# Ten raw weight buffers, five for low parts, and both weight sums loaded a pair of blocks ahead, in a decoder trunk on one core

## The chip, the core and the metric

The kernel runs on one core of a Trainium2 chip, in one launch. The time is that of the device, in microseconds (us), for the whole program. TensorE (PE) multiplies, VectorE (DVE), ScalarE (ACT) and GpSimd (POOL) do the elementwise work, and SyncE (SP) issues most DMAs. 16 DMA engines move the data.

## The reference

All is float32: 256 tokens, model width 1024, two layers, FFN width 2816. Cut to what matters:

```python
def swiglu(x, w_in, w_out):
    gate, up = jnp.split(x @ w_in, 2, axis=-1)
    return (jax.nn.silu(gate) * up) @ w_out

for layer in range(2):
    x = x + 0.5 * rms_norm(swiglu(rms_norm(x, g[0]), w_ffn_in[layer, 0], w_ffn_out[layer, 0]), g[1])
    h = rms_norm(x, g[2])
    h = mlstm_mixer(h, ...) if layer == 0 else diff_attention(h, k_sh, v_sh, ...)
    x = x + rms_norm(h, g[3])
    x = x + 0.5 * rms_norm(swiglu(rms_norm(x, g[4]), w_ffn_in[layer, 1], w_ffn_out[layer, 1]), g[5])
    gate = jax.nn.sigmoid(rms_norm(x, g[6]) @ w_ple_gate[layer])
    x = x + rms_norm((p[layer] @ w_ple_proj[layer]) * gate, g[7])
    if layer == 0:
        k_sh, v_sh = shared_kv(x, kv_norm, w_kv)      # rms_norm, then a 1024x2048 product
```

Each of the four FFNs reads 1024 x 5632 weights in and 2816 x 1024 out; mLSTM and attention read a few million more. Every weight is read from memory once or twice and used for 256 tokens only, so the weights pass through the core in a stream.

## The kernel before

**Split products.** TensorE multiplies in a format with fewer bits (fp32r). A weight block of 128 x 2048 floats (1 MB) is loaded into a *raw buffer* (`wraw`), ScalarE copies it to a *high part* (`whi`), VectorE subtracts that from the raw block and writes the *low part* (`wlo`); `parts` does both. The activations are split alike (`xh`, `xl`, for the hidden values `hh`, `hl`). A product is then three matmuls (`mm3`): high by high, low by high, high by low. There are `NRAW` = 9 raw buffers, and `NPART` = 6 each for high and for low parts. Each buffer takes 8 KB of every partition.

**Pairs of blocks.** `block_pair` computes the products of two input-weight blocks at once with seven instead of eight products, in the manner of Strassen and Winograd. `src` is the pair's first block, `src2` its second, each in two halves of 1 MB. Two of the seven weights are sums that the DMA makes: t3 = `src2[0] + src2[1]` and u1 = `src[0] + src2[0]`. For each, SyncE loads the one term (the *base load*) into a raw buffer, and then GpSimd issues an *adding load*, a DMA that adds the other term to what is there; it has to wait until the base has landed. The three blocks b11 = `src[0]`, b21 = `src[1]` and b22 = `src2[1]` are loaded plainly, and VectorE adds two more weights in place, wt2 = b11 + t3 and wt4 = b21 + b11. So a pair holds five raw buffers, and each is free when its last reader on VectorE is done. The products come in the order w11, w21, wt2, wu1, then wt3 and w22, then wt4.

**Where the pairs are.** An FFN has 11 input blocks (`NJ`); the first FFN makes pairs at 5, 7 and 9, the other three at 1, 3, 5, 7 and 9. `ffn` walks through them; between two pairs it issues the output products of the pair before (`stage_out`, weights `ffn_out`). The pairs of mLSTM (two calls) know nothing of one another. Within an FFN the next pair's t3 is loaded by the current call, between its loads of b22 and of the output weights, and handed on; u1 is loaded by the pair itself.

**What sets the order.** Nothing is issued as the code stands. The class `Notes` records all instructions, and `play` lays them in time with a model of costs: always the one that can start first, among those that could start at once the one that stands first in the code (with `is_urgent` ones before others on ACT, DVE and POOL, and SyncE strictly in the code's order among those whose buffers exist). Buffers of a kind are given out in the code's order, too, at the time when the model says that an older one is free. The result is a fixed order on each engine. `later` sets when a load counts as landed in the model, and so, when its readers may be put in place:

```python
        def later(q, t):
            t += 810 + SLACK if q.kw.get("accum_op") is not None else 180 + LATE
```

`LATE` is 600 ns, `SLACK` 3000 ns. The chip doesn't know this model: there each engine takes its instructions in that order, and waits by semaphores for what is really late. SyncE waits in the same way: a load whose buffer isn't free holds up all loads behind it. Because all instructions are issued in one place, all have the line L432 (L433 after the change).

Of the kernel before, what the change touches and what calls it, by code (L numbers as in the profile page):

```python
# [10 lines left out]
F32R = mybir.dt.float32r  # L11
# [5 lines left out]
P = 128  # L17
# [7 lines left out]
PEN = 30  # L25
MARGIN = 300
SLACK = 3000
LATE = 600
LANES = 8
DEPTH = 2  # L30
HA = 4
# [2 lines left out]
BIG = 2.0 ** 100  # L34
GKV = 8
ATT = 8
NRAW = 9
NPART = 6
NX = 7
NSG = 3  # L40
NH = 3
# [393 lines left out]
def trunk(nc, a):  # L435
# [34 lines left out]
        nc.vector.scalar_tensor_tensor(dst_lo, src, gc, dst_hi.bitcast(F32), op0=ALU.mult, op1=ALU.subtract)  # L470

    def part():
        return T([P, 2048], "whi", NPART, F32R), T([P, 2048], "wlo", NPART, F32R)


    def pair(*shape):
# [237 lines left out]

    def block_pair(xts, xf, src, src2, use, end=False, between=None, nxt=None, t3=None):
        def load(src, plus=None):
            raw = T([P, 2048], "wraw", NRAW)
            nc.sync.dma_start(raw, src)  # L720
            if plus is not None:
                nc.gpsimd.dma_start(raw, plus, accum_op=ALU.add)
            return raw

        def parts(raw):
            p_ = part()
            split(*p_, raw)
            return p_

        def add(out, v0, v1):  # L730
            nc.vector.tensor_tensor(out, v0, v1, op=ALU.add)
            return parts(out)

        nc.is_urgent = False
        if t3 is None:
            t3 = load(src2[0], src2[1])
        u1 = load(src[0], src2[0])
        b11 = load(src[0])
        w11 = parts(b11)
        b21 = load(src[1])  # L740
        w21 = parts(b21)
        wt2 = add(b11, b11, t3)
        wu1 = parts(u1)
        wt3 = parts(t3)
        b22 = load(src2[1])
        t3 = load(nxt[1][0], nxt[1][1]) if nxt else None
        w22 = parts(b22)
        wt4 = add(b21, b21, b11)
        nc.is_urgent = True

        def times(acc_, x_, w, more):
            for kk in range(4):
                c = slice(kk * 512, (kk + 1) * 512)
                mm3([acc_], x_[0][:, kk, :], x_[1][:, kk, :], [w[0][:, c]], [w[1][:, c]],
                    not more and kk == 0, kk == 3, more)

        def quarter(t, q):
            return xts[t][0][:, q:q + 4, :], xts[t][1][:, q:q + 4, :]

        def held(acc_):  # L760
            c = piece()
            nc.scalar.activation(c, acc_, AF.Copy)
            return c

        ax, ay = acc_in(), acc_in()
        times(ax, quarter(0, 0), w11, False)
        p1 = held(ax)
        times(ay, quarter(0, 4), w21, False)
        nc.vector.tensor_tensor(p1, ay, p1, op=ALU.add)
        use(0, 0, p1)  # L770
        if between:
            between()
        s1, s2, s3, n4 = xf() if callable(xf) else xf
        times(ax, s2, wt2, True)
        u2 = held(ax)
        az = acc_in()
        times(az, s1, wu1, False)
        z5 = held(az)
        if end:
            times(az, n4, w22, True)  # L780
            nc.vector.tensor_tensor(u2, az, u2, op=ALU.subtract)
            use(1, 0, u2)
        times(ax, s3, wt3, True)
        u3 = held(ax)
        nc.vector.tensor_tensor(z5, z5, u3, op=ALU.subtract)
        if not end:
            times(az, n4, w22, True)
            nc.vector.tensor_tensor(u2, az, u2, op=ALU.subtract)
        use(1, 1, z5)
        times(ax, quarter(1, 4), wt4, True)  # L790
        if not end:
            use(1, 0, u2)
        use(0, 1, ax)
        return t3

    def ffn(l, f, xts, rs, xfs, epilogue, first=None):
        acc = [None, None]
        wi, wo, hT = dict(enumerate(first)) if first else {}, {}, {}  # L800
        res = [None, None]
        gbc = []
        win = a["ffn_in"][l, f]


        def hidden(j, t, src):
            h = T([P, 256], "sg", NSG)
            nc.scalar.activation(h, src[:, :256], AF.Silu, scale=rs[t])
            nc.vector.scalar_tensor_tensor(h, src[:, 256:], rs[t], h, op0=ALU.mult, op1=ALU.mult)
            hh = T([P, 2, P], "hh", NH, F32R)  # L810
            hl = T([P, 2, P], "hl", NH, F32R)
            pt = trp()
            for i in range(2):
                nc.tensor.transpose(pt[:, i * P:(i + 1) * P], h[:, i * P:(i + 1) * P], ident)
            split(hh, hl, pt[:, :256].rearrange("p (k t) -> p k t", t=P))
            hT[j, t] = hh, hl

        def stage_in(j, t):
            if j not in wi:
                wi[j] = in_weights(win[j], m=2 if j < 2 or j == NJ - 1 else 1)  # L820
            pi = acc_in()
            in_block(pi, xts[t], wi[j])
            hidden(j, t, pi)

        def stage_out(j, t):
            if j not in wo:
                wo[j] = [weight(a["ffn_out"][l, f, j], m=2 if j < 2 or j == NJ - 1 else 1)]
            if acc[t] is None:
                acc[t] = acc_out()
            hh, hl = hT.pop((j, t))  # L830
            for i in range(2):
                out_chunk(acc[t], hh[:, i, :], hl[:, i, :], wo[j], i,
                          j == 0 and i == 0, j == NJ - 1 and i == 1)

        def end(t):
            post(t, acc[t], gbc[0], 0.5)
            res[t] = epilogue(t)

        xf = []
        first_n = 1 if first else 0  # L840
        if first:
            pis = [acc_in() for _ in range(NT)]
            for k in range(KD):
                hi, lo = wi[0][k // 4]
                c = slice(k % 4 * 512, k % 4 * 512 + 512)
                for t in range(NT):
                    mm3([pis[t]], xts[t][0][:, k, :], xts[t][1][:, k, :], [hi[:, c]], [lo[:, c]], k == 0, k == KD - 1)
            for t in range(NT):
                hidden(0, t, pis[t])
        starts = PAIRS[2 * l + f]  # L850
        items = []
        j = 1 if first else 0
        while j < NJ:
            items.append((j, j + 1) if j in starts else (j,))
            j += len(items[-1])

        begin = 0
        while len(items[begin]) == 1 and begin < (1 if first else 2):
            begin += 1

        split_begin = begin == 1 and not first
        for t in range(1 if split_begin else NT):
            for (j,) in items[:begin]:
                stage_in(j, t)
        last = [0] * first_n + [j for i in items[:begin] for j in i]
        for t in range(1 if split_begin else NT):
            stage_out(last[0], t)
        last = last[1:]

        def late():  # L870
            stage_in(0, 1)
            stage_out(0, 1)

        def all_forms():
            if not xf:
                xf.extend(forms(xfs, urgent=split_begin))
            return xf

        def both(item, **kw):
            return block_pair(xts, all_forms, win[item[0]], win[item[1]], lambda b, t, src: hidden(item[b], t, src), **kw)  # L880

        t3 = None
        for n, item in enumerate(items[begin:-1]):
            if len(item) == 2:
                nxt = items[begin + n + 1]
                t3 = both(item, between=late if split_begin and n == 0 else None, t3=t3,
                          nxt=[win[i] for i in nxt] if len(nxt) == 2 else None)
            else:
                for t in range(NT):
                    stage_in(item[0], t)  # L890
            for t in range(NT):
                for i in last:
                    stage_out(i, t)
            last = item
        item = items[-1]
        gbc.append(load_gbc(a["norm_g"][l, 4 * f + 1]))
        if len(item) == 1:
            j, = item
            stage_in(j, 0)
            for i in last:  # L900
                stage_out(i, 0)
            stage_out(j, 0)
            end(0)
            stage_in(j, 1)
            for i in last:
                stage_out(i, 1)
            stage_out(j, 1)
            end(1)
        else:

            both(item, end=True, t3=t3)
            for t in range(NT):
                for i in last:
                    stage_out(i, t)
            for t in range(NT):
                for i in item:
                    stage_out(i, t)
                end(t)
        return res
# [583 lines left out]
```

## Time and profile before

| | |
|---|---|
| time before, three runs | 1010.15, 1009.94, 1007.89 us; median 1009.94 |
| time of the profiled execution | 1006.51 us, 3.43 under the median |
| its span in the profile | 1004.7 us, TensorE's clock 0.999 of full speed |
| instructions | 12418 |
| data moved | 274.68 MB, 273 GB/s over the span |
| TensorE, VectorE, ScalarE, GpSimd busy | 987.2, 893.1, 697.9, 88.6 us |

How to read it: busy time is the time in which an engine executes; loads of weights into TensorE (PEld) overlap its matmuls. `<-` reads "made from": `whi_0r<-wraw` is a high part made from a raw buffer. Names of buffers end in a number of the buffer, which tells nothing of what is in it. In brackets stands the idle time of the engine just ahead of the instruction and what ended it. PEclk is the clock that the throttle granted TensorE; the DMA share is that of the 16 engines, and can read slightly above 1. By the tiles of the timeline the stages lie roughly so, in us from the start of the span: first FFN of layer 0 to 200, mLSTM to 300, second FFN to 472, gate and shared K/V to 495, first FFN of layer 1 to 700, attention to 785, last FFN to 966, gate to the end; the next stage's first work overlaps the one before.

### The profile page before, as it was taken

What the parts mean: (1) busy time and instruction counts of PE and PEld (TensorE: products, weight loads), DVE (VectorE), ACT (ScalarE), POOL (GpSimd) and SP (SyncE); (2) the same over time, 40 slices, a digit from 0 to 9 for tenths busy, and PEclk for the clock granted to TensorE, in tenths of its full rate; (3) what the DMA queues carried; (4) which work ended last, traced back from release to release, by engine and by line L of the source; (5) the groups of instructions that cost most, each with busy time, mean ns of one, the idle gap of its engine ahead of it and who ended that gap; (6) DMA issues with size and microseconds to landing.
All of it is one profiled execution on the core that took longest, in us unless ns stands there. A gap on an engine that the chain in (4) does not pass through costs nothing. (4 is left out here: it accounts for less than half of the span.)

```text
span 1004.7 us, 12418 instructions
## 1 busy us (share of the span) xinstructions
PE 987.2 (98%) x4636; PEld 803.2 (80%) x4636; DVE 893.1 (89%) x909; ACT 697.9 (69%) x924; POOL 88.6 (9%) x126
## 2 busy tenths in 40 slices
PE   9999999999999999999999999999999999999997
PEld 7888888887787788888887788788888887888886
DVE  6977998788999999998899899998985999999983
ACT  8747767577847867595767767676776787767662
POOL 0000000100131000001120000000002300000010
PEclk9999999999999999999999999999999999999999
DMA  9999778765699999966799999965657898998721
GB/s 345 418 333 335 234 245 301 241 191 186 252 292 339 290 337 311 311 252 221 293 280 321 349 335 326 311 248 222 232 216 230 241 330 285 286 306 283 282 84 42
DMA packets 45860, 274.68 MB, mean 273 GB/s; under 512 B 5481, under 2 KB 5865, under 8 KB 16105
## 3 DMA queue, kind: packets, MB, share of 16 engines
q1 hardware_dynamic: 39752, 231.69, 60.1%
q0 software_dynamic: 5760, 41.95, 20.8%
q8 instruction: 36, 0.59, 0.2%
q10 hardware_dynamic: 288, 0.27, 0.1%
q14 instruction: 24, 0.19, 0.0%
HBM read 263.40 MB, written 10.49 MB: 273 GB/s over the span
## 5 line engine op out<-in xcount | busy, mean ns | idle before, releaser
L432 DVE TENSOR_TENSOR wraw<-wraw,wraw 128x2048 f32<-128x2048 f32 x40 | 91.3, 2282 | 0.2
L432 ACT ACTIVATE whi_0r<-wraw 128x2048 fp32r<-128x2048 f32 (+2 forms) x49 | 77.8, 1597 | 11.7 <-DMA wraw<-in_mlstm_in 3.8
L432 ACT ACTIVATE whi_2r<-wraw 128x2048 fp32r<-128x2048 f32 (+1 forms) x48 | 79.4, 1663 | 7.7 <-PE accI L432 3.5
L432 ACT ACTIVATE whi_1r<-wraw 128x2048 fp32r<-128x2048 f32 (+2 forms) x51 | 78.2, 1542 | 7.4 <-PE accO L432 4.1
L432 ACT ACTIVATE whi_5r<-wraw 128x2048 fp32r<-128x2048 f32 (+1 forms) x44 | 71.7, 1641 | 15.6 <-PE accI L432 11.5
L432 ACT ACTIVATE whi_4r<-wraw 128x2048 fp32r<-128x2048 f32 (+1 forms) x45 | 73.7, 1648 | 6.0 <-PE accO L432 2.6
L432 ACT ACTIVATE whi_3r<-wraw 128x2048 fp32r<-128x2048 f32 (+1 forms) x45 | 74.1, 1648 | 4.9 <-DMA wraw<-in_ffn_in 3.3
L432 ACT ACTIVATE att<-accI 128x512 f32<-128x512 f32 x80 | 47.5, 593 | 34.0 <-PE accI L432 33.7
L432 POOL DMA_DIRECT2D wraw<-in_ffn_in x36 | 32.0, 888 | 426.3 <-DMA wraw<-in_ffn_in 363.3
L432 DVE TENSOR_TENSOR wlo_0r<-wraw,whi_2r 128x2048 fp32r<-128x2048 f32 (+1 forms) x25 | 48.3, 1942 | 1.3 <-ACT whi_2r L432 1.3
L432 DVE TENSOR_TENSOR wlo_3r<-wraw,whi_1r 128x2048 fp32r<-128x2048 f32 (+1 forms) x25 | 48.4, 1941 | 1.1 <-ACT whi_1r L432 1.1
L432 DVE TENSOR_TENSOR wlo_2r<-wraw,whi_2r 128x2048 fp32r<-128x2048 f32 (+1 forms) x21 | 43.7, 2080 | 4.6 <-ACT whi_2r L432 4.5
L432 DVE TENSOR_TENSOR wlo_1r<-wraw,whi_1r 128x2048 fp32r<-128x2048 f32 (+2 forms) x26 | 44.4, 1709 | 3.5 <-ACT whi_1r L432 3.4
L432 DVE TENSOR_TENSOR wlo_1r<-wraw,whi_0r 128x2048 fp32r<-128x2048 f32 (+1 forms) x23 | 46.0, 2005 | 0.4 <-ACT whi_0r L432 0.2
L432 DVE TENSOR_TENSOR wlo_0r<-wraw,whi_0r 128x2048 fp32r<-128x2048 f32 (+2 forms) x24 | 44.1, 1839 | 0.8 <-ACT whi_0r L432 0.6
L432 DVE TENSOR_TENSOR wlo_5r<-wraw,whi_4r 128x2048 fp32r<-128x2048 f32 (+1 forms) x23 | 44.0, 1912 | 0.3 <-ACT whi_4r L432 0.3
L432 DVE TENSOR_TENSOR wlo_4r<-wraw,whi_4r 128x2048 fp32r<-128x2048 f32 (+1 forms) x22 | 43.6, 1991 | 0.3 <-ACT whi_4r L432 0.3
L432 POOL TENSOR_TENSOR sm<-sm,mhalf 128x1 f32<-128x1 f32 (+2 forms) x40 | 32.5, 813 | 109.0 <-DVE sm L432 106.5
L432 DVE TENSOR_TENSOR wlo_2r<-wraw,whi_3r 128x2048 fp32r<-128x2048 f32 (+1 forms) x22 | 41.7, 1894 | 0.3 <-ACT whi_3r L432 0.3
L432 DVE TENSOR_TENSOR wlo_4r<-wraw,whi_5r 128x2048 fp32r<-128x2048 f32 (+1 forms) x22 | 41.4, 1894 | 0.0
L432 POOL TENSOR_SCALAR sm<-sm 128x1 f32<-128x1 f32 x32 | 16.9, 527 | 261.8 <-ACT sg L432 261.8
L432 ACT ACTIVATE sg<-accI,sm 128x256 f32<-128x256 f32 x34 | 16.0, 471 | 32.9 <-PE accI L432 24.2
(617 smaller groups left out, 3041.4 us busy)
## 6 DMA issues: line engine op xcount, KB each, us to landing
wraw<-in_ffn_in SPq DMA_DIRECT2D x102, 1024.0 KB, 9.5
wraw<-in_ffn_out SPq DMA_DIRECT2D x44, 1024.0 KB, 9.3
wraw<-in_ffn_in POOLq DMA_DIRECT2D x36, 1024.0 KB, 12.0
wraw<-in_mlstm_in SPq DMA_DIRECT2D x14, 1024.0 KB, 6.9
wraw<-in_ple_gate SPq DMA_DIRECT2D x8, 1024.0 KB, 5.5
wraw<-in_w_kv SPq DMA_DIRECT2D x8, 1024.0 KB, 5.1
home<-wraw SPq DMA_DIRECT2D x28, 256.0 KB, 4.1
wraw<-home SPq DMA_DIRECT2D x14, 512.0 KB, 3.4
```

The lines of the kernel that those rows point to most:

```text
L432: getattr(getattr(self.nc, eng), name)(*args, **kw)
```

## The change

Four things are changed together. There is one raw buffer more (ten) and one low-part buffer less (five; `NLOW` is new, high parts keep six): the memory is the same. A plain load counts as landed 400 ns later in the planner's model (`LATE` 1000). And in `block_pair` the sums of the next pair are no longer t3 alone, loaded ahead of `w22 = parts(b22)`, but t3 and u1 together, loaded behind it. mLSTM's pairs pass no next pair on, and so there only the numbers have an effect.

```diff
-LATE = 600
+LATE = 1000
-NRAW = 9
+NRAW = 10
 NPART = 6
+NLOW = 5
     def part():
-        return T([P, 2048], "whi", NPART, F32R), T([P, 2048], "wlo", NPART, F32R)
+        return T([P, 2048], "whi", NPART, F32R), T([P, 2048], "wlo", NLOW, F32R)
-    def block_pair(xts, xf, src, src2, use, end=False, between=None, nxt=None, t3=None):
+    def block_pair(xts, xf, src, src2, use, end=False, between=None, nxt=None, ahead=None):
...
-        if t3 is None:
-            t3 = load(src2[0], src2[1])
-        u1 = load(src[0], src2[0])
+        t3, u1 = ahead or (load(src2[0], src2[1]), load(src[0], src2[0]))
         b11 = load(src[0])
         w11 = parts(b11)
         b21 = load(src[1])
...
         b22 = load(src2[1])
-        t3 = load(nxt[1][0], nxt[1][1]) if nxt else None
         w22 = parts(b22)
+        ahead = (load(nxt[1][0], nxt[1][1]), load(nxt[0][0], nxt[1][0])) if nxt else None
         wt4 = add(b21, b21, b11)
...
-        return t3
+        return ahead
```

(`ffn` hands `ahead` on in the place of `t3`.) The instructions are the same ones, 12418 before and after; what moves is their place on each engine, and the buffers that they use. Three places follow; `wraw_8_85` is a raw buffer, the second number only an address in the order.

SyncE at the last pair of FFN one of layer 1, before: t3, two blocks of output weights, the gains of a norm, two halves of a parked residual (`home`), u1, then b11, b21 and b22.

```order
L432 DMA wraw_8_85<-in_ffn_in 128x2048
L432 DMA wraw_5_82<-in_ffn_out 128x2048
L432 DMA wraw_7_84<-in_ffn_out 128x2048
L432 DMA wraw_6_83<-in_norm_g 128x1024
L432 DMA wraw_2_79<-home_2_88 128x1024
L432 DMA wraw_2_79<-home_3_89 128x1024
L432 DMA wraw_1_78<-in_ffn_in 128x2048
L432 DMA wraw_4_81<-in_ffn_in 128x2048
L432 DMA wraw_3_80<-in_ffn_in 128x2048
L432 DMA wraw_5_82<-in_ffn_in 128x2048
```

And after:

```order
L433 DMA wraw_0_76<-in_ffn_in 128x2048
L433 DMA wraw_1_77<-in_ffn_in 128x2048
L433 DMA wraw_4_80<-in_ffn_out 128x2048
L433 DMA wraw_7_83<-in_ffn_out 128x2048
L433 DMA wraw_9_85<-in_norm_g 128x1024
L433 DMA wraw_5_81<-home_2_88 128x1024
L433 DMA wraw_5_81<-home_3_89 128x1024
L433 DMA wraw_8_84<-in_ffn_in 128x2048
L433 DMA wraw_3_79<-in_ffn_in 128x2048
L433 DMA wraw_6_82<-in_ffn_in 128x2048
```

u1 has moved up five places, right behind t3; b11, b21 and b22 keep theirs.

VectorE from the attention to the start of the last FFN, before (`xl`: low part of the activations; `sm4` and `mhalf`: the statistics of the softmax's norm; `accO`: an accumulator; the sums into `wraw_8_85` and `wraw_5_82` are the residual):

```order
L432 TENSOR_TENSOR wlo_4r_75<-wraw_0_77,whi_5r_70 128x1024
L432 TENSOR_TENSOR wlo_1r_72<-wraw_4_81,whi_0r_65 128x1024 x2
L432 SCALAR_TENSOR_TENSOR sm4_4_138<-sm4_2_136,sm4_0_134 128x2
...
L432 SCALAR_TENSOR_TENSOR xl_2r_115<-tr_0_97,sub_0_164,xh_2r_108 128x512
L432 SCALAR_TENSOR_TENSOR wraw_5_82<-wraw_8_85,sm1_4_160,wraw_5_82 128x512 x2
L432 TENSOR_TENSOR wlo_2r_73<-wraw_2_79,whi_3r_68 128x1024
L432 TENSOR_TENSOR att_4_102<-tr_0_97,gcol_0_130 128x512
L432 TENSOR_TENSOR att_1_99<-accI_2_92,gcol_0_130 128x512
L432 TENSOR_TENSOR xl_0r_113<-att_4_102,xh_0r_106 128x512
L432 TENSOR_TENSOR xl_4r_117<-att_1_99,xh_4r_110 128x512
L432 TENSOR_TENSOR wlo_2r_73<-wraw_2_79,whi_3r_68 128x1024
```

And after:

```order
L433 TENSOR_TENSOR wlo_0r_71<-wraw_7_83,whi_1r_66 128x1024 x2
L433 SCALAR_TENSOR_TENSOR sm4_4_138<-sm4_2_136,sm4_0_134 128x2
...
L433 SCALAR_TENSOR_TENSOR xl_2r_115<-tr_0_97,sub_0_164,xh_2r_108 128x512
L433 SCALAR_TENSOR_TENSOR wraw_1_77<-wraw_4_80,sm1_4_160,wraw_1_77 128x512 x2
L433 TENSOR_TENSOR wlo_2r_73<-wraw_3_79,whi_4r_69 128x1024
L433 TENSOR_TENSOR att_7_105<-tr_0_97,gcol_0_130 128x512
L433 TENSOR_TENSOR att_2_100<-accI_1_91,gcol_0_130 128x512
L433 TENSOR_TENSOR xl_0r_113<-att_7_105,xh_0r_106 128x512
L433 TENSOR_TENSOR xl_4r_117<-att_2_100,xh_4r_110 128x512
L433 TENSOR_TENSOR wlo_2r_73<-wraw_3_79,whi_4r_69 128x1024
L433 TENSOR_TENSOR wlo_3r_74<-wraw_0_76,whi_0r_65 128x1024 x2
```

The low part `wlo_1r` of before, ahead of the softmax's statistics, is the `wlo_2r` of after, one half behind the residual sum and one behind `xl`; what was there before (`wlo_2r` of before) follows it as `wlo_3r`.

GpSimd in the attention, before: an adding load (for t3), two powers of the softmax's norm, the next adding load (for u1).

```order
L432 TENSOR_TENSOR sm4_1_135<-sm4_13_147,mhalf_0_133 128x4
L432 DMA wraw_6_83<-in_ffn_in 128x2048
L432 TENSOR_TENSOR sm4_3_137<-sm4_4_138,mhalf_0_133 128x2
L432 TENSOR_TENSOR sm4_5_139<-sm4_9_143,mhalf_0_133 128x2
L432 DMA wraw_1_78<-in_ffn_in 128x2048
```

And after:

```order
L433 TENSOR_TENSOR sm4_1_135<-sm4_13_147,mhalf_0_133 128x4
L433 DMA wraw_9_85<-in_ffn_in 128x2048
L433 DMA wraw_5_81<-in_ffn_in 128x2048
L433 TENSOR_TENSOR sm4_3_137<-sm4_4_138,mhalf_0_133 128x2
L433 TENSOR_TENSOR sm4_5_139<-sm4_9_143,mhalf_0_133 128x2
```

The second adding load, with its wait for the base to land, now stands ahead of the two powers.

More of the change, by code (lines that the diff above doesn't have):

```diff
@@ L880, in both @@
             return block_pair(xts, all_forms, win[item[0]], win[item[1]], lambda b, t, src: hidden(item[b], t, src), **kw)
-        t3 = None
+        ahead = None
         for n, item in enumerate(items[begin:-1]):
@@ L885, in ffn @@
                 nxt = items[begin + n + 1]
-                t3 = both(item, between=late if split_begin and n == 0 else None, t3=t3,
-                          nxt=[win[i] for i in nxt] if len(nxt) == 2 else None)
+                ahead = both(item, between=late if split_begin and n == 0 else None, ahead=ahead,
+                             nxt=[win[i] for i in nxt] if len(nxt) == 2 else None)
             else:
@@ L909, in ffn @@
         else:
-            both(item, end=True, t3=t3)
+            both(item, end=True, ahead=ahead)
             for t in range(NT):
```

## The prediction

> **What bounds the kernel now.** I read the page's busy shares and slices first, then the busy time of TensorE by stretch, then the chain of waits, then the timeline at each place where TensorE stood idle.
>
> ```profile
> PE 987.2 (98%) x4636; PEld 803.2 (80%) x4636; DVE 893.1 (89%) x909; ACT 697.9 (69%) x924; POOL 88.6 (9%) x126
> DMA  9999778765699999966799999965657898998721
> ```
>
> TensorE works 98% of the span. Both programs hold the same instructions, so its 987.2 us stay, and the change can only touch the 17.5 us in which it stands still. The busy time by stretch (us, PE busy and count, granted clock, DMA share, GB/s) says where these lie:
>
> ```profile
> 0.00:25.00 25.00, 23.12 (x98) 1.00 0.92 344
> ...
> 225.00:300.00 75.00, 72.71 (x339) 1.00 0.72 243
> 300.00:325.00 25.00, 24.93 (x114) 1.00 1.02 332
> 325.00:350.00 25.00, 22.73 (x100) 1.00 0.96 301
> ...
> 500.00:575.00 75.00, 73.89 (x341) 1.00 0.97 314
> 575.00:650.00 75.00, 75.00 (x338) 1.00 0.97 319
> 650.00:675.00 25.00, 24.01 (x109) 1.00 0.65 254
> ...
> 825.00:875.00 50.00, 48.48 (x216) 1.00 0.93 276
> 875.00:975.00 100.00, 100.00 (x461) 1.00 0.71 249
> 975.00:1004.70 29.70, 22.34 (x123) 0.96 0.17 60
> sum 1004.70, PE 987.17; mean PE 75.94
> ```
>
> 1.88 us go at the start and 7.36 us in the tail, where no pair of blocks is loaded: the change leaves both. That leaves 17.53 - 9.24 = 8.29 us: mLSTM 2.29, the start of the second FFN of layer 0 (300 to 350) 2.34, the start of the first FFN of layer 1 (500 to 575) 1.11, its last pair (650 to 675) 0.99, the start of the last FFN (825 to 875) 1.52, and 0.04 elsewhere. Two of the five are on the chain of waits with a landing:
>
> ```profile
> 635.70 2.21 DVE wraw L432
> 637.93 10.85 DMA wraw<-in_ffn_in
> 648.80 1.92 ACT whi_3r L432
> ...
> 835.68 10.50 DMA wraw<-in_ffn_in
> 846.26 1.92 ACT whi_3r L432
> ```
>
> VectorE's sum of two blocks ends and frees a raw buffer, the load that waited for it is issued, it lands 10.9 us later, and ScalarE rounds it. So at these places the supply of raw buffers sets the time of a product, and a tenth buffer or another order of loads bears on it. Where it is not the load, it is VectorE:
>
> ```profile
> 290.00:350.00 60.00, 58.76 (x56) 1.00 1.00 310
> 500.00:550.00 50.00, 48.44 (x53) 1.00 0.96 298
> ...
> 764.00:783.00 19.00, 8.10 (x16) 1.00 1.01 294
> 783.00:852.00 69.00, 66.95 (x64) 1.00 0.89 282
> ```
>
> These are VectorE's busy times (same columns): 98% and 97% at three FFN starts, but idle for more than half of the stretch just ahead of the last one, in the attention.
>
> **The change part by part.** All is counted against the profiled execution, 1006.51 us, of which the span is 1004.7; the median of the three runs is 1009.94, 3.43 above it, and I add that at the end.
>
> *The tenth raw buffer.* SyncE's queue is in order and its loads of weights stand waiting for a buffer most of the time, and so a tenth buffer lets each load go one release earlier:
>
> ```profile
> SPq L432 <- DVE wraw L432: 143.3, 48, 17.1
> ...
> L432 DVE TENSOR_TENSOR wraw<-wraw,wraw 128x2048 f32<-128x2048 f32 x40 | 91.3, 2282 | 0.2
> ```
>
> (VectorE's releases by sums alone held the queue 143.3 us in 48 waits; a sum takes 2.28 us, and so does a low part.) One release is therefore worth at least 2.28 us of an earlier issue where VectorE runs without a gap, and nothing where PE isn't waiting for a load.
>
> *mLSTM, second pair of blocks: forecast -2.0.* The pair's first block waits for its load:
>
> ```profile
> 220.07 0.86 POOL L432 DMA_DIRECT2D wraw<-in_mlstm_in  x1 [2.92 <-DMA wraw<-in_mlstm_in]
> 221.02 8.93 SPq L432 DMA_DIRECT2D wraw<-in_mlstm_in  x3
> ...
> 233.10 1.92 ACT L432 ACTIVATE whi_0r<-wraw 128x2048 fp32r<-128x2048 f32 x1 [3.83 <-DMA wraw<-in_mlstm_in]
> ...
> 235.53 0.69 DVE L432 TENSOR_TENSOR att<-att,att 128x512 f32<-128x512 f32 x1 [3.76 <-ACT att L432]
> ```
>
> It was issued at 221.0, 1 us behind an adding load of POOL, and ScalarE could start at 233.10, after 3.83 us of waiting; VectorE then waited 3.76 us. Issued one release earlier, the block comes 2.3 us earlier or more and goes ahead of that adding load, not behind it. The new order of TensorE also has the products there in unbroken groups of twelve matmuls, where the old one cut them up to fill the wait. Bounds: 0 (another operand is late, at the same time) to -2.29 (all of the stretch's idle time). I take -2.0, near the far end, since the wait of 3.83 us is longer than the idle time it makes. There is nothing loaded ahead in this stage, so the other half of the change has no part in it.
>
> *Last pair of the first FFN of layer 1: forecast -1.0.* Here both weight sums are loaded a pair ahead. SyncE's order moves the load of u1 five places up, past two blocks of the output weights and three small loads; the two block loads b11 and b21 then stand in front of nothing but their own buffers.
>
> ```profile
> 636.75 0.86 POOL L432 DMA_DIRECT2D wraw<-in_ffn_in  x1 [17.47 <-DMA wraw<-in_ffn_in]
> ...
> wraw<-in_ffn_in SPq DMA_DIRECT2D x102, 1024.0 KB, 9.5
> wraw<-in_ffn_in POOLq DMA_DIRECT2D x36, 1024.0 KB, 12.0
> wraw<-in_mlstm_in POOLq DMA_DIRECT2D x4, 1024.0 KB, 12.4
> ...
> q1 hardware_dynamic: 39752, 231.69, 60.1%
> q0 software_dynamic: 5760, 41.95, 20.8%
> ```
>
> The critical b21 (637.93, 10.85 us) ran beside the adding load of u1 (636.75), against a median of 9.5 us from issue to landing. An adding load takes 20.8/41.95 = 0.50% of the engines per MB, a plain one 60.1/231.69 = 0.26%: 1.9 times. Loaded a pair ahead, u1's adding load is out of b21's way, and b21 itself goes a release (2.28 us) earlier. Either is more than the 0.99 us of idle time. The two output blocks that u1 passes are wanted only after the pair. Bounds 0 to -0.99; I take -1.0.
>
> *Second FFN of layer 0: forecast -0.5.*
>
> ```profile
> 340.69 0.50 PE L432 MATMUL accI<-whi_1r,xh_1r 128*128 128x512 f32 x1 [1.14 <-ACT whi_1r L432]
> ...
> 342.08 0.50 PE L432 MATMUL accI<-wlo_4r,xh_2r 128*128 128x512 f32 x1 [0.89 <-DVE wlo_4r L432]
> ```
>
> TensorE waits first for a high part, then for a low part, with VectorE 98% busy for 60 us. An earlier landing can't give VectorE time; what the change does is swap two low parts of that pair and take one sum forward. Bounds 0 to -2.34, and I stay near the low end, because VectorE's rows decide here and its work is the same.
>
> *First FFN of layer 1, its start: 0.* DMA stands at 0.97 and VectorE at 97%. The tenth buffer brings loads forward by one release, the fifth low buffer in place of the sixth holds low parts back by one. Bounds -1.11 to +2.28 (one low part uncovered).
>
> *Five low buffers, the last FFN: forecast +0.5.* A low part can be written only when TensorE has read an older one out. With a lead of many products that costs nothing; at the start of the last FFN there is none: TensorE waits for low parts that VectorE has just made.
>
> ```profile
> 764.68 2.50 DVE L432 TENSOR_TENSOR wlo_1r<-wraw,whi_0r 128x1024 fp32r<-128x1024 f32 x2
> ...
> 850.68 0.50 PE L432 MATMUL accO<-wlo_5r,hh_1r 128*128 128x512 f32 x1 [1.15 <-DVE wlo_5r L432]
> ```
>
> The two halves of the sixth low part (2.50 us at 764.68, in the attention's idle stretch of VectorE, 8.10 of 19 us busy) now stand behind the residual sums at 783, in the stretch that is 97% busy. So 2.5 us of work come into 69 us that had 2.05 us free. On the other side the loads of this FFN come one release earlier and a sum that was made early is put off, which is what TensorE waited for at 841 to 852. Bounds -1.52 (all idle time gone) to +2.5 (the shifted work uncovered). The middle is +0.5, and I take that.
>
> *POOL in the attention: 0.* The adding load of the second weight sum moves ahead of two small powers:
>
> ```profile
> 767.85 0.71 POOL L432 TENSOR_TENSOR sm<-sm,mhalf 128x2 f32<-128x2 f32 x1 [5.04 <-DVE sm L432]
> ...
> 769.84 0.92 POOL L432 DMA_DIRECT2D wraw<-in_ffn_in  x1
> ```
>
> POOL waits there for the base load to land. If that lands after 767.85 the softmax of the attention waits with it; if not, the issue of 0.92 us fits into the 5.04 us that POOL idled. The base's load goes up the queue by three or more releases, so I put it at nothing; its price if the cover is gone is 0.92 us and what the base is late.
>
> Everywhere else (25 to 225, 350 to 500, 575 to 650, 675 to 825, 875 to 975) TensorE has no gap: earlier loads hide there, as the moved loads of output weights do. *The later landings in the order* (the 1000 in place of 600) only set which instruction stands first on each queue; their effect is in the moves above.
>
> Sum: -2.0 - 1.0 - 0.5 + 0 + 0.5 + 0 = -3.0. 1006.51 - 3.0 = 1003.5 for an execution like the profiled one; 3.43 more is 1006.9.
>
> **The rivals.** *Larger gain.* All 8.29 us between start and tail go, as each place is fed earlier: 1009.94 - 8.29 = 1001.7; half of the remainder beyond my sum gives 1004.3. For it: every wait of TensorE listed above is short (0.9 to 1.2 us), less than one release. Against: VectorE at 97 to 98%.
>
> *Nothing gained.* VectorE sets the FFN starts and an earlier landing turns into a longer wait in a buffer; only the last pair of layer 1 and part of mLSTM pay, and the last FFN loses as much: within 1.5 us of 1009.9, 1008.4 to 1011.4.
>
> *Slower: the low parts.* At each of the three FFN starts with VectorE at 97 to 98% (290, 500, 783), one low part of 2.28 us that was made in a gap ahead of it falls into the full stretch. This decides as soon as the stretch has less than 2.28 us free, and they have 1.24 of 60, 1.56 of 50 and 2.05 of 69 us (the rows above). If TensorE pays for each in full, 3 x 2.28 = 6.8; less the 2.0 and 1.0 that the loads still bring, 1013.7. Against it: the low parts' lead outside these starts, and that two of three places have sums pushed back in exchange.
>
> *Slower: the adding loads.* Both weight sums ahead mean two adding loads back to back in front of the next pair's blocks. An adding load costs 0.208 x 1004.7 / 40 = 5.2 us of all engines (20.8% for the 40 of them, by the rows of 36 in the FFN and 4 in mLSTM at 1 MB each), a plain one 2.6. Where engines are full (1.02 at 300 to 325) the blocks behind land up to 5.2 us later. One release of 2.28 us is gained, 2.9 lost; at the three starts with no lead 3 x 2.9 = 8.7 at most, half of it on the path +4.4, less the 1.0 of the last pair: 1013.3. It speaks against it that u1 was loaded in front of b11 before as well, and only its place among other loads moves. The Trainium skill, page "DMA: Bandwidth & Descriptors", section "Queues, rings and completion order", says that each engine takes packets in turn from the queues that have work. By that rule an early adding load slows every plain load beside it, wherever it is put. The trace agrees at 637.93, where b21 took 10.85 us beside an adding load; by that rule the last pair would gain and a start with full engines lose, which is this rival's 1013.3.
>
> **How the numbers follow.** 0.3% is 3.0 us, about what a measurement of this kernel tells from no change; the line for faster is 1006.9, for slower 1013.0. The forecast (1005.4 to 1008.4) 0.40, half of it below the line; larger gain 0.25, faster; nothing gained 0.17; low parts 0.13 and adding loads 0.05, both slower. Faster 0.20 + 0.25 = 0.45, same 0.20 + 0.17 = 0.37, slower 0.18. The predicted time is that of the forecast, 1006.9. The range runs from 1002.0, near the full gain of 1001.7, to 1013.0, which leaves out most of the two slower cases (some 0.16) and 0.03 at the lower end. The forecast's own range is 1005.4 to 1008.4, and cases without a real gain hold 0.35.
>
> **What the profile would show.** Right: in mLSTM no wait of ScalarE for a landing near 233 and 225 to 300 with under 1 us idle; no landing of 10.85 us on the chain near 638 and 650 to 675 full; TensorE's total as before, 987; SyncE's waits for VectorE's releases shorter or shifted to low buffers. Wrong: new waits of TensorE for low parts at 500 to 550 or 783 to 860, or ScalarE waiting for landings at 300 to 340 or near 800, or POOL's powers late at 768. The forecast fails if the idle time at the starts of FFNs grows by more than mLSTM and the last pair give back, that is if VectorE is a bound in those 60 us that can't take even 2.5 us more.

## The result, and the profile after

The changed kernel took 1002.72 us (median of 4 runs, 1002.19 to 1003.52) against 1008.91 us; the ratio of the runs is 0.9935, 95% interval 0.9919 to 0.9951. A second set of 6 runs (1001.94 to 1004.14) gave 0.9925 (0.9906 to 0.9943). By these ratios it is 6.6 to 7.6 us faster, where 3 were forecast; the time lies in the range. The two profiled executions differ by only 3.9 us (1006.51 and 1002.59 us). That is the first thing to explain. (One of the 12 runs of a kernel below, the one with the 400 ns alone, took 1098.73 us at a mean granted clock of 0.848; medians and ratios leave it out.) The profile after counts 12442 instructions, not the 12418 of before that the part on the change gives for both; those that keep the engines busy are the same in number (4636 matmuls, 909 on VectorE, 924 on ScalarE, 126 on GpSimd).

TensorE's busy time by stretch, after (us, PE busy and count, granted clock, DMA share, GB/s):

```profile
225.00:300.00 75.00, 74.52 (x352) 1.00 0.76 257
300.00:325.00 25.00, 23.88 (x108) 1.00 1.03 340
325.00:350.00 25.00, 24.62 (x111) 1.00 1.01 327
350.00:500.00 150.00, 149.76 (x683) 1.00 0.78 273
500.00:575.00 75.00, 74.70 (x346) 1.00 1.01 318
575.00:650.00 75.00, 75.00 (x340) 1.00 0.98 346
650.00:675.00 25.00, 25.00 (x112) 1.00 0.64 234
...
825.00:875.00 50.00, 47.67 (x212) 1.00 0.98 314
875.00:975.00 100.00, 99.72 (x456) 1.00 0.64 221
...
sum 1000.80, PE 986.40; mean PE 75.88
```

Idle time of TensorE, before, after and forecast:

| stretch | before | after | change | forecast |
|---|---|---|---|---|
| mLSTM, 225 to 300 | 2.29 | 0.48 | -1.81 | -2.0 |
| start of the second FFN of layer 0, 300 to 350 | 2.34 | 1.50 | -0.84 | -0.5 |
| 350 to 500 | 0.00 | 0.24 | +0.24 | 0 |
| start of the first FFN of layer 1, 500 to 575 | 1.11 | 0.30 | -0.81 | 0 |
| its last pair, 650 to 675 | 0.99 | 0.00 | -0.99 | -1.0 |
| start of the last FFN, 825 to 875 | 1.52 | 2.33 | +0.81 | +0.5 |
| 875 to 975 | 0.00 | 0.28 | +0.28 | 0 |

Together -3.1; TensorE's busy time reads 0.77 lower for the same matmuls (987.17 and 986.40; their ends are modelled), which makes the 3.9 us. So profile against profile the sum (-3.0) is nearly right. The other 3 us lie between the profiled execution of before and its median.

In mLSTM the loads stand where the prediction put them: the queue goes on at 208 instead of 210.7, both adding loads of POOL go earlier, the first block's load is issued at 214.0 instead of 221.0, now ahead of the second adding load, and the block that was rounded at 233.10 is rounded 8 us sooner.

```profile
208.09 18.32 SPq L433 DMA_DIRECT2D wraw<-in_mlstm_in  x5
...
216.74 0.86 POOL L433 DMA_DIRECT2D wraw<-in_mlstm_in  x1 [2.22 <-DMA wraw<-in_mlstm_in]
...
225.04 1.91 ACT L433 ACTIVATE whi_0r<-wraw 128x2048 fp32r<-128x2048 f32 x1
...
232.50 1.92 ACT L433 ACTIVATE whi_1r<-wraw 128x2048 fp32r<-128x2048 f32 x1 [2.23 <-DMA wraw<-in_mlstm_in]
```

One sign that the prediction named is not met: ScalarE still waits for a landing near 233, 2.23 us, now for the next block. TensorE hardly notices (0.48 us idle in the stretch). One of its signs of being wrong did show: TensorE waits at 832 for a low part (1.03 us), as it had at 850 before (1.15).

### The profile page after: what moved, and what is told of

The parts are those of the page before. It is cut to its first block, busy times and chain, and to the rows that moved or that the text cites. A ratio compares the mean times of both kernels' runs of the same rounds, so it can differ in the third digit from the quotient of the medians.

```text
span 1000.8 us, 12442 instructions
## 1 busy us (share of the span) xinstructions
PE 986.4 (99%) x4636; PEld 803.0 (80%) x4636; DVE 892.8 (89%) x909; ACT 698.6 (70%) x924; POOL 94.9 (9%) x126
## 4 chain that ended last, share of the span: by engine, by line
PE 47%; issue 2%; ACT 2%; POOL 1%; DVE 1%; DVEq 0%; POOLq 0%; ACTq 0%
PE accI L433 30%; PE accO L433 15%; PE tr L433 2%; POOL sm L433 1%; ACT sg L433 1%; DVE wlo_4r L433 0%; ACT att L433 0%; DVE wlo_2r L433 0%; ACT wraw L433 0%; ACT whi_5r L433 0%; ACT whi_0r L433 0%; DVE wraw L433 0%; DVE att L433 0%; DVE xl_5r L433 0%; DVEq L1498 0%
## 5 line engine op out<-in xcount | busy, mean ns | idle before, releaser
L433 ACT ACTIVATE sg<-att,sm 128x256 f32<-128x256 f32 x54 | 26.9, 502 | 16.9 <-DVE att L433 16.8
L433 ACT ACTIVATE sg<-accO 128x512 bf16<-128x512 f32 (+2 forms) x46 | 20.2, 445 | 25.0 <-PE accO L433 21.0
L433 PEld LDWEIGHTS tr<-ident,sg 128*128 128x128 f32 x176 | 23.0, 140 | 14.6 <-DVE hl_2r L433 2.7
L433 PE MATMUL tr<-ident,sg 128*128 128x128 f32 x176 | 34.0, 274 | 0.3 <-DVE hl_2r L433 0.3
L433 DVE SCALAR_TENSOR_TENSOR wraw<-wraw,sm,wraw 128x512 f32<-128x512 f32 x32 | 22.7, 749 | 12.0 <-POOL sm L433 11.9
L433 DVE TENSOR_TENSOR att<-accI,att 128x512 f32<-128x512 f32 x40 | 27.4, 685 | 3.3 <-PE accI L433 2.9
L433 ACT ACTIVATE sg<-wraw 128x512 bf16<-128x512 f32 x32 | 20.1, 630 | 13.7 <-DVE wraw L433 9.7
L433 ACT ACTIVATE att<-accI,sm 128x512 f32<-128x512 f32 (+1 forms) x22 | 14.8, 671 | 20.8 <-PE accI L433 20.8
L433 DVE SCALAR_TENSOR_TENSOR sg<-att,sm,sg 128x256 f32<-128x256 f32 x54 | 25.7, 480 | 1.7 <-ACT sg L433 1.5
L433 DVE TENSOR_TENSOR att<-att,att 128x512 f32<-128x512 f32 (+1 forms) x33 | 22.4, 679 | 3.8 <-ACT att L433 3.6
```

What stands on the lines that cost most here:

```text
L433: getattr(getattr(self.nc, eng), name)(*args, **kw)
```

## The experiments

**Where the spread of before comes from.** The kernel before, as a second program.

> The kernel before, unchanged, as a second program. Its profiled execution took 1006.51 us and its four runs had a median of 1008.91, while the changed kernel's profiled run stood at its median. Theory 1 (some of the time before is in landings that come late by a different amount each time): this kernel's runs spread over 2 us or more, its profile has other idle times of TensorE at 225-300, 500-575 and 825-875 than the first profile (a difference of 0.5 us or more in one of them), ratio 1.000 within 0.002. Rival (the first profiled run was only a lucky draw of the whole chip, no place in it): idle times place by place within 0.2 us of the first profile.

12 runs from 1006.42 to 1013.63 us, ratio 0.9999 (0.9983 to 1.0016); its profiled run took 1007.93. The idle times of places that wait for a landing differ from the first profile: 0.78 in place of 0.50 us at 235, 1.47 in place of 0.99 at 651, and a new 0.45 at 689; those that wait for VectorE or ScalarE alone agree to 0.03 (1.14 and 0.89 at 340). Ratio and spread are as theory 1 had them. The places are so in part only: in the three stretches that it named the idle time differs by 0.26 us at most, less than its 0.5, and the differences of about 0.5 lie at 651 and 689. All of this is far from 7 us.

A second candidate for the spread showed in profiles of the next kernels. With the buffers alone TensorE waited 1.95 us at 337, and then:

```profile
335.00:340.00 5.00, 3.05 (x15) 1.00 1.02 329
340.00:345.00 5.00, 5.00 (x18) 0.66 0.94 267
345.00:350.00 5.00, 4.99 (x22) 1.00 1.00 267
```

The granted clock stood at 0.66 for 5 us: 5 x 0.34 = 1.7 us are lost, on top of the wait. Below, such a fall of the granted clock is called a closing. The kernel with only the 400 ns changed had a waiting stretch at 270 and lost as much behind it, 5 x 0.18 + 5 x 0.17 = 1.75:

```profile
270.00:275.00 5.00, 2.02 (x7) 0.82 0.37 107
275.00:280.00 5.00, 5.00 (x20) 0.83 0.92 385
```

The Trainium skill, page "TensorE: Matmul & The Clock Gate", Part 1, has the clock gate at half rate after an idle window, and the windows free-running, of about 3.4 us each. The trace agrees in the size: half of 3.4 is the 1.7 us of a closing. It differs in what closes the gate: the wait of 1.95 us here is shorter than such a window, and the measurement decides. A free-running window would fit that the same waits of 1.14 and 0.89 us at 340 closed the gate in one execution (sums ahead alone, clock 0.93 in 325 to 350) and not in three others (before, twice, and five low buffers alone with 1.13 and 0.90); no run shows the windows themselves.

Neither profiled run of before had a closing ahead of its last matmul, so that closings take part in its spread is inferred. Over 83 runs of that kernel the mean clock points that way: 14 runs at 0.999 took 1005.9 to 1009.0 us (median 1007.7), 62 at 0.996 to 0.998 had a median of 1009.6, and 7 at 0.994 or 0.995 took 1012.0 to 1013.6. (The mean is a rough sign only: the clock also falls in the tail, after the last matmul, which costs nothing. The profile of the changed kernel reads 0.997 with no other closing.)

**The parts alone.** Ten and five buffers and nothing else (the low parts take `NLOW`, as in the change):

```diff
-NRAW = 9
+NRAW = 10
 NPART = 6
+NLOW = 5
```

> Ten raw buffers and five low ones, nothing else of the change. Theory 1 (the supply of raw buffers is what paid): mLSTM loses 1.8 us of idle time as in the changed kernel, the FFN starts gain about 1, the last pair of the first FFN of layer 1 gains its 1.0 as b21 goes a release earlier; ratio 0.995 to 0.997. Rival (the move of u1 paid, buffers are hidden): only mLSTM's 1.8 goes, ratio 0.998 or above.

1005.29 us, ratio 0.9961 (0.9943 to 0.998): theory 1's number. mLSTM idles 0.78 us, the last pair not at all. But the start of the second FFN of layer 0 idles more than before (2.92 us, and the closing above comes on top), which theory 1 did not have.

Both sums ahead, with the old numbers (the other lines of `block_pair` as in the change):

```diff
-        t3 = load(nxt[1][0], nxt[1][1]) if nxt else None
         w22 = parts(b22)
+        ahead = (load(nxt[1][0], nxt[1][1]), load(nxt[0][0], nxt[1][0])) if nxt else None
```

> t3 and u1 both loaded a pair ahead, behind the split of b22; nine raw, six low buffers and 600 ns kept. Theory 1: mLSTM as before (2.3 us idle at 225-300, since no pair is loaded ahead there), the last pair of the first FFN of layer 1 without its 1.0 us, the FFN starts at most 0.5 better: ratio 0.997 to 1.000; holding u1 a pair longer in one of nine buffers takes one from the others, so a loss of up to 2 us is possible. Rival (the move of u1 paid): ratio 0.993 to 0.996.

1008.07 us, 0.9985 (0.9972 to 0.9998), as theory 1 had it: the last pair's 1 us is gone, mLSTM's is not (3.1 us idle). Its 12 runs spread over 2.9 us only, although it has waits of 1.31 and 1.14 us and a closing in its profile; so the length of the waits alone doesn't set the spread.

The planner's 400 ns alone (`LATE = 1000`):

> Only the planner's landing later by 400 ns. Theory 1: it alone moves single instructions by one or two places, ratio 0.998 to 1.002, mLSTM's idle time within 0.5 us of the 2.3 before. Rival (the order, not the buffers, took the waits away, as the products of mLSTM stand in whole groups of twelve after the change): mLSTM loses over 1 us, ratio 0.995 to 0.998.

1009.89 us (11 runs), 1.0009 (0.9995 to 1.0023): no gain, theory 1. mLSTM idled 5.4 us in the profiled run (1014.23 us, two closings), which theory 1 did not expect.

**Taking parts away from the change.** By the products of these ratios the whole should be 0.9961 x 0.9985 x 1.0009 = 0.9955, and it is 0.9935 and 0.9925, a difference that these intervals alone don't settle. First the changed kernel again, for its spread:

> The changed kernel once more, for its spread. Theory 2, formed on the first four runs: the spread of the kernel before (1005.9 to 1013.5 us in 31 runs) is made of idle times of TensorE that are long enough for the clock gate to close, each closing costing 1.7 us (profiles with one: 0.66 for 5 us at 340), on top of landings that come late by a varying amount; the changed kernel has no idle time of over 1.1 us between start and tail, so it spreads over less than 3 us and stays under 1005.5 in every run: ratio 0.992 to 0.995. Rival (the spread is the chip's, whatever the kernel): 12 runs spread over 5 us or more, up to 1008.

1003.04 us, 0.9925 (0.9906 to 0.9943), all runs between 1001.94 and 1004.14: theory 2, on 6 runs. The profile has no closing between start and tail.

Without the 400 ns (`LATE = 600`):

> The changed kernel with landings planned at 600 ns as before; buffers and both sums ahead kept. Buffers alone gave 0.9961, sums alone 0.9985, the 400 ns alone 1.0009. Theory 1 (the parts add up, the 400 ns are worth nothing): 0.9946, and idle times as in the changed kernel within 0.5 us. Rival (the 400 ns pay where loads come earlier, since with the buffers alone TensorE waited 1.95 us at 337 and the changed kernel didn't): 0.996 to 0.998, with a wait of over 1.5 us at 337 or 830.

1008.51 us, 0.9985 (0.9972 to 0.9998): the parts do not add up, theory 1 falls here. Without the 400 ns nearly the whole gain is gone. It waits at 337 just as the kernel with the buffers alone, and once more at 353 (1.40). In its profile TensorE idles 8.6 us between 225 and 975, against 5.2 in the changed kernel's, and the gate closes once at 835: 3.4 and 1.7 of the 5.7 us between these two profiled executions. In the kernel with the buffers alone the place at 337 reads:

```profile
336.76 0.48 ACT L433 ACTIVATE sg<-accI,sm 128x256 f32<-128x256 f32 x1 [1.45 <-PE accI L433]
337.40 1.91 ACT L433 ACTIVATE whi_5r<-wraw 128x2048 fp32r<-128x2048 f32 x1
...
339.36 0.50 PE L433 MATMUL accI<-whi_5r,xh_1r 128*128 128x512 f32 x1 [1.95 <-ACT whi_5r L433]
```

ScalarE waits 1.45 us for TensorE to end a product, with the rounding of the next weight queued behind, and then TensorE waits 1.95 us for that rounding. In the changed kernel 325 to 350 idles 0.38 us: the planner, with landings put 400 ns later, laid out another order of products there. TensorE goes on with products of `whi_3r`, rounded early, and takes none of `whi_5r` before 346:

```profile
331.13 1.91 ACT L433 ACTIVATE whi_3r<-wraw 128x2048 fp32r<-128x2048 f32 x1
...
336.47 1.91 ACT L433 ACTIVATE whi_5r<-wraw 128x2048 fp32r<-128x2048 f32 x1
```

Nine and six buffers (with sums ahead and 400 ns):

> The changed kernel with nine raw and six low buffers again. Theory 1 (parts add up): 0.9985 x 1.0009 = 0.9994, mLSTM idle by 2 us or more with a wait for a landing near 235, last pair of the first FFN of layer 1 without idle time. Rival (sums ahead and 400 ns are most of the gain together): 0.995 to 0.997.

1009.52 us, 0.9997 (0.9984 to 1.001), as theory 1 had it. mLSTM idles 4.95 us: it waits at 235 again (1.25 us), and at 270 for a low part (2.15 us). Its profile has two closings.

t3 alone ahead, at its old place, the rest of the change kept:

```diff
-        t3, u1 = ahead or (load(src2[0], src2[1]), load(src[0], src2[0]))
+        if t3 is None:
+            t3 = load(src2[0], src2[1])
+        u1 = load(src[0], src2[0])
...
+        t3 = load(nxt[1][0], nxt[1][1]) if nxt else None
         w22 = parts(b22)
-        ahead = (load(nxt[1][0], nxt[1][1]), load(nxt[0][0], nxt[1][0])) if nxt else None
```

> The changed kernel with t3 alone loaded ahead, at its old place; ten raw, five low buffers and 1000 ns kept. Theory 1 (parts add up): 0.9961 x 1.0009 = 0.9970. Rival (with ten buffers u1's place no longer matters, and the 400 ns were what was missing): 0.993 to 0.995, the idle time of the last FFN's start 1.5 us or less against 2.3 in the changed kernel.

1003.77 us, 0.9933 (0.9914 to 0.9951): the rival. Beside ten buffers and the 400 ns, u1's place is worth 0.7 us by the medians (1003.77 and 1003.04), within what these runs can tell from nothing.

**The low buffers.** Five in place of six, nothing else (`NLOW = 5`, nine raw):

> The kernel before with five low buffers in place of six and nothing else: the price of the buffer that was given up. The prediction put it at +0.5 us at the start of the last FFN (bounds -1.5 to +2.5), with a rival of 2.28 us at each of three FFN starts. Theory 1 (a low part has leads of many products nearly everywhere): ratio 0.999 to 1.002, the idle time at 825-875 within 1 us of the 1.5 before. Rival: 1.004 to 1.007, with waits of TensorE for low parts of over 2 us at 340, 540 or 840.

1006.67 us, 0.9975 (0.9962 to 0.9987): faster, which neither theory had. The start of the last FFN does idle 0.82 us more (2.34), so the forecast's +0.5 was near; the gate closed there as well in this profile (0.68 in 835 to 840), 1.7 us that the forecast didn't have. But mLSTM's wait of 3.83 us for a landing is 0.65, the start of the first FFN of layer 1 idles 0.29 in place of 1.11, and the last pair there doesn't idle, although its load is as late as before. ScalarE at that place, first this kernel, then the one before:

```profile
645.45 0.36 ACT L433 ACTIVATE hh_1r<-tr 128x256 fp32r<-128x256 f32 x1
648.73 1.92 ACT L433 ACTIVATE whi_3r<-wraw 128x2048 fp32r<-128x2048 f32 x1 [2.92 <-DMA wraw<-in_ffn_in]
```

```profile
648.80 1.92 ACT L432 ACTIVATE whi_3r<-wraw 128x2048 fp32r<-128x2048 f32 x1 [2.14 <-DMA wraw<-in_ffn_in]
650.62 0.36 ACT L432 ACTIVATE hh_1r<-tr 128x256 fp32r<-128x256 f32 x1
...
651.49 0.44 PE L432 MATMUL tr<-ident,sg 128*128 128x128 f32 x2 [0.99 <-DVE hl_2r L432]
...
663.01 0.39 PE L432 MATMUL accI<-whi_3r,xh_1r 128*128 128x512 f32 x1
```

The block lands at 648.7 in both; ScalarE waits even longer for it with five low buffers. What held TensorE was not that block, of which it took the first product at 663.0 only: it was the small copy `hh_1r` that stood behind the waiting `whi_3r` in ScalarE's queue, by way of VectorE's `hl_2r` and the single transposing accumulator `tr`. Put ahead of it, the copy is done at 645.8, and the late load costs nothing. Where the copy stands behind, the landing sets the stall: ScalarE waited 2.14, 2.55 and 3.04 us for the block in the profiles of before, of its second run and of the 400 ns alone, and TensorE then 0.99, 1.47 and 1.89. (The same form of stall comes up at 682 instead, 0.96 us, where VectorE waits 1.35 us for a small load with TensorE's operand behind.)

By the ratios the five low buffers alone bring 2.5 us, and ten and five together 3.9. The intervals overlap, and no run has ten raw and six low buffers, so what the tenth raw buffer is worth by itself isn't shown.

Eleven and four:

> The changed kernel with eleven raw and four low buffers. Theory 1 (where loads set the time, a release earlier pays; where low parts do, it costs): mLSTM has nothing left to gain (0.4 us idle), the last FFN's start waits longer for low parts than the 2.1 us of the changed kernel: 0.993 to 1.000. Rival (more raw buffers pay on): under 0.992.

1027.61 us, 1.0184 (1.0168 to 1.02): slower than theory 1 had it (0.993 to 1.000). The waits for low parts come back, and the gate closes four times; once it stays at half rate beyond one window:

```profile
PE accI L433 <- DVE wlo_0r L433: 3.4, 5, 1.8
PE accI L433 <- DVE wlo_2r L433: 3.2, 3, 2.3
```

```profile
220.00:225.00 5.00, 2.24 (x11) 1.00 0.81 146
225.00:230.00 5.00, 4.89 (x16) 0.65 1.00 346
230.00:235.00 5.00, 5.00 (x12) 0.50 0.35 147
235.00:240.00 5.00, 5.00 (x20) 0.83 0.00 0
```

That one costs 5 x (0.35 + 0.50 + 0.17) = 5.1 us; with the three others at 1.7 it makes 10 of the some 25 us by which this kernel is slower than the changed one.

**Two attempts to go further.** u1 ahead in the first three FFNs only (`both_sums=2 * l + f < 3`), to take the two waits of 1 us away at 830:

> The changed kernel, but the last FFN loads only t3 a pair ahead, at its old place; the other three keep both sums. With t3 alone everywhere the last FFN's start had waits of 0.69, 0.42 and 0.43 us, with both sums 1.09 and 1.00. Theory 3 (u1's adding load stands in front of loads that the last FFN's start needs): 0.991 to 0.9925, no wait of 0.9 us or more at 800-850, under the changed kernel by 0.3 to 1 us. Rival (the move of u1 is worth nothing anywhere, 0.9933 against 0.9925 is noise): 0.9925 to 0.994.

1002.82 us, 0.9937 (0.9924 to 0.995), level with the changed kernel's 1002.72 and 1003.04, and the waits at 829 and 831 (1.07 and 1.03) are still there: theory 3 falls, u1 in the last FFN isn't their cause. The same two waits closed the gate in this profile and not in the changed kernel's; first the changed kernel, then this one:

```profile
830.00:835.00 5.00, 2.90 (x13) 1.00 1.04 298
```

```profile
830.00:835.00 5.00, 3.56 (x8) 0.68 0.95 185
```

So the changed kernel carries that risk as well.

Another 400 ns (`LATE = 1400`):

> The changed kernel with landings planned another 400 ns later. Theory 4 (the planner put products too early because it thought landings 0.4 to 2 us earlier than the chip has them; a later plan is safer still): 0.990 to 0.993, no wait over 1 us between start and tail. Rival (1000 ns was enough to turn one order at 337, a further step just deals new orders, some with new waits): 0.993 to 0.999, with another wait of over 1 us somewhere.

1005.74 us, 0.9964 (0.9951 to 0.9976): the rival. New waits of 1.29 and 1.24 us at 337 and 352. So 1000 is no threshold past which plans are safe; each value deals another order. No version was faster than the changed kernel.

## Why the prediction was right in sign and short in size

The time of 1002.72 us lies 0.7 above the lower end of the range. That the sum fits the two profiles to 0.1 us is in part luck: single places are off by up to 0.8 us, and these errors cancel.

- **mLSTM, -2.0: right**, -1.81, with the block ahead of the second adding load as said, and with the tenth raw buffer: with ten the idle time there is 0.2 to 0.8 us in seven profiles that differ otherwise (five low buffers in all of them), with nine and six 2.3 to 5.4 in five. Nine and five gave 1.7, so the low buffers have a part in it, and how the two share it isn't shown; why the same load landed 3.5 us earlier there (rounded at 229.61, from the same place in the queue) stays open.
- **Last pair, -1.0: the size was right, the reason was half of it.** The prediction read the chain (sum, landing, rounding) as if the rounded block was what TensorE wanted. That one it took 12 us later; it wanted the small copy queued behind. An earlier load takes the stall away (sums ahead alone), but so does the copy's place in the queue (five low buffers alone), with the load as late as ever.
- **Second FFN of layer 0, -0.5: too small** (-0.84), and the argument that VectorE's rows decide there was wrong in part: what moves the idle time at 337 is which product the fixed order asks for next, and ScalarE's queue (1.95 us with ten buffers and 600 ns, 0 with 1000).
- **First FFN of layer 1, 0: wrong**, -0.81. Five low buffers alone give -0.82; I had those as a cost there. Why they help isn't shown.
- **Last FFN, +0.5: right in sign**, +0.81, and +0.82 with five low buffers alone. What the two waits can cost beyond that, a closing, was not in it.
- **POOL in the attention, 0: right.** No gap of TensorE opens in 675 to 825 (149.95 us busy before and after).
- **"The later landings only set the order; their effect is in the moves above": the step that failed.** That was no term of the sum at all. Alone the 400 ns are worth nothing (1.0009), beside the other parts the gain from 0.9985 to 0.9925.
- **"3.43 more": the other step that failed.** I carried the distance from the profiled execution of before to its median over as a constant. It isn't one. Landings that vary (0.5 us at single places of before) and closings of the clock gate behind idle times, 1.7 us each, would make such a distance; in the kernel before the closings are inferred from mean clocks. The changed kernel's profiled run stood at its own median (1002.59 and 1002.72). So those 3 us of the gain were not read from a profile without closings, though the quoted runs (1006.51 against 1009.94) hinted at them. That waits of this length carry such a risk is shown; how much of the 3 us is closings and how much landings is not, since only one execution of each program has a trace.
- The rivals: "larger gain" gave 1001.7 to 1004.3, where the measured time lies too, but not by its mechanism: 5.2 us of idle time between start and tail are still there, of 8.29. "Low parts" was wrong at five; at four (with eleven raw buffers) its waits came, and the time went far past its 1013.7, to 1027.61. "Adding loads" is not seen: with both sums ahead the start of the second FFN of layer 0 got no worse, and u1's place made no difference with ten buffers.

## What to carry to other kernels

Before a stall is put down to a late load, look at what stands behind the waiting instruction in its engine's queue: a 0.36 us copy there cost 1 us, and with the copy ahead the stall was gone, the load as late as before. Where a planner fixes the order, buffers, order and its latency numbers can't be priced one by one (0.9961, 0.9985 and 1.0009 alone, 0.9985 without the last, 0.9925 together). And where TensorE is 98% busy, compare the profiled execution with the spread of the runs first: waits of some 2 us, in one piece or two, can cost another 1.7 us through the clock.

## What the runs showed of the hardware that was not expected

Short waits of TensorE closed its clock gate, in some executions and not in others. A single wait of 1.95 us closed it with the buffers alone and not in the change without the 400 ns; waits of 1.89 and 2.32 us closed it in other kernels, single waits of up to 1.62 us in no profile. Two waits of 1.03 to 1.07 us within 2 us closed it in three kernels (five low buffers alone, u1 ahead in three FFNs, and the change without the 400 ns), and the like, 1.00 to 1.09 us, not in the changed kernel, twice, nor with 1400 ns. The traces have 13 closings ahead of the last matmul: 12 cost 1.7 to 1.75 us each, and one, behind a wait of 2.01 us, 5.1.

The 83 runs of the kernel before spread over 7.7 us (1005.9 to 1013.6), and one set of 12 alone over 7.2; those of the changed kernel, whose longest wait is 1.1 us, over 2.2 (1001.94 to 1004.14, ten runs). Since the sums ahead alone, with waits of 1.3 us, spread over 2.9, the cause of the difference stays open.
